# Hybrid decoder trunk: gate matmuls in fewer portions, keys and diagonal solves at later steps, T1's four products piece by piece

## The chip, the core and the metric

The kernel runs on one core of one Trainium2 chip. The metric is the device time in microseconds (us) of one execution. The core has a matrix engine (TensorE, here PE, whose weight loads are listed as PEld), VectorE (DVE), ScalarE (ACT), GpSimd (POOL) and SyncE (SP, which here only issues DMAs). Each engine works through its own list of instructions in a fixed order and waits on semaphores for the others.

## The reference

One layer of a decoder on 512 prompt tokens and 8 sample tokens, all in float32, model width 2048:

```
xn = rmsnorm(h);  proj = xn @ w_in            # q | k | v | z | beta logits | decay logits | pool channels
q, k, v = silu(short_conv(...)); l2norm(q), l2norm(k)
beta = sigmoid(b_raw);  g = -exp(a_log) * softplus(a_raw + dt_bias)
o = gated delta rule(q, k, v, cumsum(g), beta)   # per head: unit lower triangular solve in each chunk
h = h + [rmsnorm(o) * silu(z) ; multiscale_pool(p)] @ w_out
xn2 = rmsnorm(h);  gu = xn2 @ w_gate_up
h = h + (silu(gu[:, :5632]) * gu[:, 5632:]) @ w_down
y = rmsnorm(h)
```

For the prompt the delta rule is computed in chunks: the decay logits g are cumulated along the tokens, a triangular matrix of key products is built for each head and chunk, and it is inverted. The sample tokens use the stored states. The new states are outputs too.

## The kernel before

**Products in three passes.** The activations stand as columns (channels on partitions, 520 tokens along the free axis). Each float32 operand is cut into a high and a low part (ACT writes the high part by a cast, DVE the low part by a subtraction: lines L146 and L148, and L1222 and L1223 later), and a product is three matmuls, high x high, high x low, low x high (L179 to L181, and in the second half L1229 to L1231 in `passes`). A product of one output tile with 16 tiles of depth is done for two halves of the tokens (264 and 256 columns) that alternate on PE, the second three tiles behind the first (`product`, L183).

**Banks.** PSUM is split into two pools: `ps_mm` with three banks for the accumulators of the big products (L79) and `ps_dn` with five banks for the rest (L80, `pst()`).

**The weave.** In the first half, small work is woven between the matmuls of the big products: `Weave` (L43) has two tracks, each a list of tasks written as generators. `product` calls `weave.step()` after each pair of half steps in which both halves are at work, and once at its end, which makes 16 steps for a product of depth 16; a step in the middle of a product has six matmuls between it and the next. A task's `yield n` lets it rest for n steps; the next task of its track begins in the step in which the one before ends, but not before its own delay. Track 1 holds, in this order, `gates()` (L560), `keys(h)` for heads 0 to 3 with a delay of 16 each (L769), `eliminate(0)` (L803), and later the same for heads 4 to 7. Heads 0 and 1 have their key products behind them when the tracks start, so the steps run through the key products of heads 2 and 3, then the z-products (`z_tile`, L1023), then the q and v products (`qv_tiles`, L1096), which add `delta(h)` (L825) to track 0. Only PE's order is that of the program in this half (L531); the other engines' lists are made when the kernel is planned, from what is estimated to be ready and, among that, by place in the program, with the casts of weights and the evictions put ahead. So an engine can be given work of a later stage early, and then holds to that order.

- `gates()`: matmuls of the beta and decay logits (L566, L567: 64 of them, weights of 32 columns), a yield after every four depth tiles, 2 steps, transposes (L574), a chain on DVE and ACT (L580 to L611, result `gtok`, in the profile `sc_g`), 13 steps, matmuls that cumulate it (L616 to L618, L627), a row per head written to DRAM (L630), 4 steps, a last small matmul (L641).
- `keys(h)`: the decay tile `dm` of the head (`decay`, L752: a DMA of the head's row to all partitions into `gcb`, DVE L758, an exponential on ACT L760; both tiles are of tag `g3`, of which there are three), the key products and transposes on PE (L775, L778), sums of squares on ACT (L766), a power on POOL (L226), scaled products on DVE (L790, L792), a yield of 4 for heads 0 to 2 and of 2 for the others, and then four DMAs that write the diagonal blocks of 32 x 32 to DRAM (L797) and four memsets of them on POOL (L800).
- `eliminate(b)`: reads the diagonal blocks of four heads (L806, tile `nb`), clears `u` on POOL (L809, L810), solves all 64 blocks at once by 31 pairs of DVE operations (L815, L817), and writes the result to DRAM (L818, L821).
- `z_tile(h)`: a product whose accumulators ACT evicts with a Silu (L1027).
- `delta(h)`: uses `decay(h)` again (L758, L760, and a second exponential, L831), and the solved blocks, read back into `utf` (L1100), on PE from L839 on; POOL copies a part (L843).

**The second half** is ordered by hand on all engines (L1439). It computes the products with Strassen's scheme: forms of the activations (B11, B21, B22, T1 to T4) are made piece by piece by `stream` (L1604), two depth tiles at a time: DVE makes the piece, ACT its high part (L1598), DVE its low part (L1602). The first two pairs of output tiles of w_gate_up (weights `w0`, `w1`) are computed plainly while the forms are being made. Around the change PE runs: a0 and a1 (products with B11, copied out by L1709 and L1720), h0 (with B21), then four products with T1 (weights A11 and A21 of `w0` into `c0[0]`, `c0[1]`, those of `w1` into `c1[0]`, `c1[1]`, L1727 to L1731), then six products with B22 and B21 (L1736 to L1747) of 24 matmuls each, and then the first steady pair `gu[2]` with its products M1 (A11 with B11), M4 (A22 with T4), M7 and so on. On DVE and ACT the same stretch of the program holds the streams of T1, B22, T3, T2 and T4 (L1718 to L1755), the cuts of the weights (`gu[1].cut("A12")` L1733, `place` L1735, `gu[2].cut("A11")` L1742, `gu[2].cut("A22")` L1758) and the outputs of the first pairs (`gate_out`, L1395, `up_out`, L1399).

Of the kernel before, what the change touches and what calls it, by code (L numbers as in the profile page):

```python
# [69 lines left out]
def decoder_kernel(ctx, tc, x_prompt, x_sample, state_delta, state_conv, state_pool, norm_mix, w_in,  # L70
# [15 lines left out]
    c1 = c1s.enter_context(tc.tile_pool(name="c1", bufs=1, side="right"))  # L86

    def pst():
        return ps_dn.tile([P, 512], F32, tag="dn", name="dn")
# [118 lines left out]
    def part(hk, half, k0=0, k1=8):  # L208
        return (mixa, mixb)[hk][:, k0:k1, HALF * half:HALF * half + HALF]
# [14 lines left out]
    def pow_mhalf(out, src):  # L224
        n = src.shape[0]
        pool.tensor_tensor(out, src, mhalf[:n, :src.shape[1]], op=ALU.pow)  # L226
# [303 lines left out]
    with ExitStack() as p1:  # L530
# [4 lines left out]
        def d1tile(tag, shape, name, dtype=F32):  # L535
            return (pre if tag == "ext" else d1).tile(shape, dtype, tag=tag, name=name, bufs=BUFS[tag])
# [23 lines left out]
        def gates():  # L560
            take = scratch("aq", "g3")
            bas = d1tile("s0", [32, NTOK], "bas")
            for c0, c1 in CHUNKS:
                pa = pst()[:32, :c1 - c0]
                for k in range(KT):
                    te.matmul(pa, wba[:, k, :], xh[:, k, c0:c1], start=(k == 0), stop=False)  # L566
                    te.matmul(pa, wba[:, k, :], xl[:, k, c0:c1], start=False, stop=(k == KT - 1))  # L567
                    if k % 4 == 3:
                        yield 1
                dve.tensor_copy(bas[:, c0:c1], pa)  # L570
            yield 2
# [5 lines left out]
            with tc.high_priority(offset=AHEAD):  # L577
# [27 lines left out]
                for c in (15.0, 13.0, 11.0, 9.0, 7.0, 5.0, 3.0):  # L605
# [4 lines left out]
                act.activation(al, al, AF.Exp)  # L610
                dve.scalar_tensor_tensor(gtok, ax, -1.0, al.rearrange("p (o h) -> p o h", o=1).broadcast_to([P, 5, H]),  # L611
                                         op0=ALU.mult, op1=ALU.mult)
            yield 13
            g4 = gtok[:, 0:4, :].rearrange("p c h -> p (c h)")
            pg = pst()
            te.matmul(pg[:, 0:32], triu, g4, start=True, stop=True)  # L616
# [112 lines left out]
        def v3(a):  # L729
            return a.rearrange("p (c j) -> p c j", c=NCH)  # L730

        def bc3(a):
            return a.rearrange("p (c o) -> p c o", o=1).broadcast_to([P, NCH, P])

        def ck(c):
            return slice(P * c, P * (c + 1))
# [15 lines left out]
        def decay(h):  # L752

            gcb = d1tile("g3", [P, SEQ], "gcb")
            sp.dma_start(gcb, gcr_d[h:h + 1, :].broadcast_to([P, SEQ]))
            dm = d1tile("g3", [P, SEQ], "dm")
            for c in range(NCH):
                dve.scalar_tensor_tensor(dm[:, ck(c)], gcb[:, ck(c)], gcs[:, c, h:h + 1], mneg,  # L758
                                         op0=ALU.subtract, op1=ALU.min)
            act.activation(dm, dm, AF.Exp)  # L760
            return gcb, dm

        def squares(src, ss):
            junk = d1tile("junk", [P, P], "junk")
            for c in range(NCH):
                act.activation(junk, src[:, ck(c)], AF.Square, accum_out=ss[:, c:c + 1])  # L766


        def keys(h):  # L769
            kT, nn = mixb[:, h % 4, 0:SEQ], mixb[:, 4 + h % 4, 0:SEQ]  # L770
            kd = kds[h] = d1tile("kd", [P, SEQ], "kd")
            _, dm = decay(h)
            gp_ = pst()
            for c in range(NCH):
                te.matmul(gp_[:, ck(c)], kT[:, ck(c)], kT[:, ck(c)], start=True, stop=True)  # L775
            ktp = pst()
            for c in range(NCH):
                te.transpose(ktp[:, ck(c)], kT[:, ck(c)], ident)  # L778
            ss = d1tile("ss", [P, NCH], "ss")
            squares(ktp, ss)  # L780
            dve.tensor_scalar(ss, ss, EPS, None, op0=ALU.add)
            rr = d1tile("rr", [P, NCH], "rr")
            pow_mhalf(rr, ss)
            fk, ik, ad = sck[:, h, 0, :], sck[:, h, 1, :], sck[:, h, 2, :]
            dve.tensor_tensor(fk, rr, rr, op=ALU.mult)
            dve.tensor_tensor(fk, fk, btok[:, 0:4, h], op=ALU.mult)
            dve.tensor_tensor(ik, ss, rr, op=ALU.mult)
            dve.tensor_tensor(ad, fk, edec[:, :, h], op=ALU.mult)
            for c in range(NCH):
                dve.scalar_tensor_tensor(nn[:, ck(c)], gp_[:, ck(c)], fk[:, c:c + 1], dm[:, ck(c)],  # L790
                                         op0=ALU.mult, op1=ALU.mult)
            dve.tensor_tensor(v3(kd), v3(ktp), bc3(ad), op=ALU.mult)  # L792
            yield 4 if h < 3 else 2
            nn3 = v3(nn)
            for q in range(4):
                r = slice(32 * q, 32 * q + 32)
                sp.dma_start(nd_d[h, q].rearrange("c s j -> s c j"), nn3[r, :, r])  # L797
            for q in range(4):
                r = slice(32 * q, 32 * q + 32)
                pool.memset(nn3[r, :, r], 0.0)  # L800


        def eliminate(b):  # L803
            hs = slice(4 * b, 4 * b + 4)
            nb = d1tile("nb", [64, 32, 32], "nb")
            sp.dma_start(nb.rearrange("p s j -> p (s j)"), nd_d[hs].rearrange("h q c s j -> (h q c) (s j)"))  # L806
            u = d1tile("u", [64, 32, 32], "u")
            uf = u.rearrange("p s j -> p (s j)")
            pool.memset(uf, 0.0)  # L809
            pool.memset(uf[:, 0:1024:33], 1.0)  # L810
            for t in range(31, 0, -1):
                w = 32 - t
                tm = d1tile("tm", [64, 256], "tm")
                tv = tm[:, 0:t * w].rearrange("p (s j) -> p s j", j=w)
                dve.tensor_tensor(tv, nb[:, 0:t, t:t + 1].broadcast_to([64, t, w]),  # L815
                                  u[:, t:t + 1, t:32].broadcast_to([64, t, w]), op=ALU.mult)
                dve.tensor_tensor(u[:, 0:t, t:32], u[:, 0:t, t:32], tv, op=ALU.subtract)  # L817
            sp.dma_start(ud_d[hs, :, 0].rearrange("h q c s j -> (h q) c (s j)"), uf)  # L818
            ut = d1tile("nb", [64, 32, 32], "ut")
            dve.tensor_copy(ut, u.rearrange("p s j -> p j s"))  # L820
            sp.dma_start(ud_d[hs, :, 1].rearrange("h q c s j -> (h q) c (s j)"), ut.rearrange("p s j -> p (s j)"))  # L821
            yield 1
# [285 lines left out]
        for b in range(2):  # L1108
            for h in range(4 * b, 4 * b + 4):
                qkv_tile(1, h, mixb[:, h % 4, 0:SEQ],  # L1110
                         {0: ext_first, 1: ext_second}.get(h))
                if h == 0:
                    weave.add(states())
                    weave.add(gates(), 1)
                weave.add(keys(h), 1, 16)
            weave.add(eliminate(b), 1)
            for h in range(4 * b, 4 * b + 4):
                z_tile(h)
            for h in range(4 * b, 4 * b + 4):
                qv_tiles(h)  # L1120
# [105 lines left out]
    def passes(acc, w, form, start=True, stop=True, ks=None):  # L1226
        (wh, wl), (xf, xg) = w, forms[form]
        for k in ks or range(wh.shape[1]):
            te.matmul(acc, wh[:, k, :], xf[:, k, :], start=start and k == 0, stop=False)  # L1229
            te.matmul(acc, wh[:, k, :], xg[:, k, :], start=False, stop=False)  # L1230
            te.matmul(acc, wl[:, k, :], xf[:, k, :], start=False, stop=stop and k == wh.shape[1] - 1)  # L1231
# [161 lines left out]
    def gate_out(i, half, a, b):  # L1393
        c = slice(HALF * half, HALF * half + HALF)
        dve.tensor_tensor(sg[:, i, c], a, b, op=ALU.add)  # L1395
        act.activation(sg[:, i, c], sg[:, i, c], AF.Silu)
# [207 lines left out]
    def stream(name, src, make, lag=1):  # L1604

        for i in range(4 + lag):
            if i < 4:
                make(2 * i)
                high(name, src, 2 * i)
            if i >= lag:  # L1610
                low(name, src, 2 * (i - lag))

    def minus(dst, a, b):
        def make(k):
            r = slice(k, k + 2)
            dve.tensor_tensor(dst[:, r, :], a[:, r, :], b[:, r, :], op=ALU.subtract)

        return make
# [64 lines left out]
    c0 = [ps_mm.tile([P, HALF], F32, tag="mm", name="mm") for _ in range(2)]  # L1683
    a0 = two()
    halves = slice(0, HALF), slice(HALF, NTOK)
    w0, w1 = gu[0].w, gu[1].w
# [37 lines left out]
    stream("B22", part(1, 1), lambda k: normed(1, 1, k, k + 2))  # L1724
    for j in range(2):
        gate_out(j, 0, sg[:, j, halves[0]], h0[j])
    passes(c0[0], w0["A11"], "T1", stop=False)  # L1727
    passes(c0[1], w0["A21"], "T1", stop=False)
    c1 = [ps_mm.tile([P, HALF], F32, tag="mm", name="mm"), pst()[:, :HALF]]
    passes(c1[0], w1["A11"], "T1", stop=False)  # L1730
    passes(c1[1], w1["A21"], "T1", stop=False)  # L1731
    stream("T3", part(0, 1), minus(part(0, 1), part(1, 1), part(0, 1)))
    gu[1].cut("A12")  # L1733
    gu[2].load("A22")
# [350 lines left out]
```

## Time and profile before

| What | us |
|---|---|
| median of three runs | 2163.61 |
| lowest and highest run | 2163.47, 2163.62 |
| the profiled execution's own time | 2163.7 |
| its span (first to last instruction) | 2161.9 |
| PE busy in it | 2135.7 |

The profile is of one execution. A row of the timeline gives the start in us from the span's start, the duration (of the whole group where instructions are merged, with their count behind an x), the engine, the line, the operation, what it writes and reads, and in brackets how long the engine had been idle before and what ended that. A row of the waits gives who waited for whom, the sum in us, how often, and the longest. Matmuls overlap, so their distance is read from start to start. `SPq` rows are DMAs being issued.

### The profile page before, as it was taken

How to read it: one execution, taken by the hardware profiler on the slowest of the kernel's cores; microseconds unless marked ns; L12 is line 12 of the kernel's file. 1: busy time of each engine (PE TensorE's matmuls, PEld its weight loads, DVE VectorE, ACT ScalarE, POOL GpSimd, SP SyncE). 2: the span in 40 equal slices, each digit the busy share in tenths (PEclk: the TensorE clock that was granted, in tenths of full speed). 3: DMA queues.
4: the chain of work that ended last, by engine and by line, in shares of the span. 5: the costliest groups of instructions: out<-in, count | busy, mean ns of one | idle time of the engine just before them, and what ended most of it. 6: DMA issues, size and time to landing. Idle time of an engine off the chain costs nothing.

```text
span 2161.9 us, 42973 instructions
## 1 busy us (share of the span) xinstructions
PE 2135.7 (99%) x17809; PEld 2128.0 (98%) x17809; DVE 1719.7 (80%) x2517; ACT 952.2 (44%) x1493; POOL 439.6 (20%) x517
## 2 busy tenths in 40 slices
PE   7999999999999999999999999999999999999998
PEld 7999999999999999999999999999999999999998
DVE  7675657656499979988889888888877898887997
ACT  6534553443264545434334334434434444435544
POOL 2201120111012212233233233232013302003100
PEclk9999999999999999999999999999999999999999
DMA  8343233323445543555455554554446746438333
GB/s 263 96 111 94 81 96 102 96 77 82 131 125 152 152 128 108 147 161 148 142 162 148 146 161 146 144 164 135 129 139 189 240 107 208 115 103 251 89 108 119
DMA packets 443808, 297.03 MB, mean 137 GB/s; under 512 B 26540, under 2 KB 424773, under 8 KB 440269
## 3 DMA queue, kind: packets, MB, share of 16 engines
q1 hardware_dynamic: 424653, 220.87, 36.4%
q0 software_dynamic: 17968, 72.77, 10.4%
q8 instruction: 139, 2.28, 0.4%
q10 hardware_dynamic: 992, 0.66, 0.1%
q14 instruction: 56, 0.46, 0.1%
HBM read 251.47 MB, written 43.43 MB: 136 GB/s over the span
## 4 chain that ended last, share of the span: by engine, by line
PE 91%; DVE 5%; ACT 1%; issue 1%; DMA 1%; POOL 0%; DVEq 0%; POOLq 0%; ACTq 0%
PE dn L1229 21%; PE dn L1230 21%; PE dn L1231 21%; PE mm L179 7%; PE mm L180 7%; PE mm L181 7%; DVE lo L1223 1%; PE dn L858 1%; DMA st<-a_d 1%; DVE raw L1251 0%; POOL st L1784 0%; PE dn L968 0%; PE dn L865 0%; PE dn L775 0%; PE dn L904 0%
## 5 line engine op out<-in xcount | busy, mean ns | idle before, releaser
L1222 ACT CAST hi<-raw 128x1024 fp32r<-128x1024 f32 (+1 forms) x422 | 427.6, 1027 | 406.0 <-DVE raw L1251 209.7
L1223 DVE TENSOR_TENSOR lo<-raw,hi 128x1024 fp32r<-128x1024 f32 (+1 forms) x422 | 525.2, 1265 | 89.5 <-ACT hi L1222 85.9
L179 PE MATMUL mm<-xh,hi 128*128 128x256 f32 (+1 forms) x1280 | 379.5, 297 | 2.3 <-ACT mixa L1027 1.4
L180 PE MATMUL mm<-xl,hi 128*128 128x256 f32 (+1 forms) x1280 | 362.0, 283 | 2.5 <-DVE xl L360 2.1
L181 PE MATMUL mm<-xh,lo 128*128 128x256 f32 (+1 forms) x1280 | 361.9, 283 | 0.0
L180 PEld LDWEIGHTS mm<-xl,hi 128*128 128x128 f32 x1280 | 242.1, 189 | 3.6 <-DVE xl L360 2.9
L179 PEld LDWEIGHTS mm<-xh,hi 128*128 128x128 f32 x1280 | 241.6, 189 | 3.4 <-ACT mixa L1027 1.6
L181 PEld LDWEIGHTS mm<-xh,lo 128*128 128x128 f32 x1280 | 241.0, 188 | 0.0
L1251 DVE TENSOR_TENSOR raw<-raw 128x1024 f32<-128x1024 f32 (+1 forms) x130 | 173.8, 1337 | 2.2
L1229 PE MATMUL dn<-b21h,hi 128*128 128x260 f32 x620 | 175.5, 283 | 0.0
L1231 PE MATMUL dn<-b21h,lo 128*128 128x260 f32 x620 | 175.5, 283 | 0.0
L1230 PE MATMUL dn<-b21l,hi 128*128 128x260 f32 x620 | 175.0, 282 | 0.4 <-DVE b21l L1794 0.4
L1231 PE MATMUL dn<-b11h,lo 128*128 128x260 f32 x612 | 173.5, 283 | 1.7 <-DVE lo L1223 1.7
L1229 PE MATMUL dn<-b11h,hi 128*128 128x260 f32 x612 | 173.3, 283 | 0.0
L1230 PE MATMUL dn<-b11l,hi 128*128 128x260 f32 x612 | 172.6, 282 | 0.0
L148 DVE TENSOR_TENSOR lo<-raw,hi 128x1024 fp32r<-128x1024 f32 (+2 forms) x86 | 101.8, 1187 | 80.7 <-ACT hi L146 80.5
L1229 PE MATMUL dn<-T1h,hi 128*128 128x260 f32 x556 | 157.9, 284 | 0.0
L1230 PE MATMUL dn<-T1l,hi 128*128 128x260 f32 x556 | 157.7, 284 | 0.0
L1231 PE MATMUL dn<-T1h,lo 128*128 128x260 f32 x556 | 156.7, 282 | 0.0
L1229 PE MATMUL dn<-B22h,hi 128*128 128x260 f32 x548 | 155.2, 283 | 0.0
L1230 PE MATMUL dn<-B22l,hi 128*128 128x260 f32 x548 | 155.0, 283 | 0.0
L1231 PE MATMUL dn<-B22h,lo 128*128 128x260 f32 x548 | 154.1, 281 | 0.4 <-DVE lo L1223 0.4
(658 smaller groups left out, 6414.3 us busy)
## 6 DMA issues: line engine op xcount, KB each, us to landing
raw<-in_w_gate_up_dram SPq DMA_DIRECT2D x134, 512.0 KB
raw<-in_w_in_dram SPq DMA_DIRECT2D x80, 512.0 KB
a_d<-mixa POOLq DMA_DIRECT2D x22, 1040.0 KB, 5.5
raw<-in_w_down_dram SPq DMA_DIRECT2D x48, 448.0 KB
mixb<-in_w_gate_up_dram SPq DMA_DIRECT2D x41, 512.0 KB
raw<-in_w_out_dram SPq DMA_DIRECT2D x25, 512.0 KB
st<-a_d POOLq DMA_DIRECT2D x49, 260.0 KB, 6.4
raw<-in_w_down_dram SPq DMA_DIRECT2D x24, 512.0 KB
```

The lines of the kernel that those rows point to most:

```text
L148: dve.tensor_tensor(lo[:, r], raw[:, r], hi[:, r].bitcast(F32), op=ALU.subtract)
L179: te.matmul(acc[ci], wh, hi[k][:, c0:c1], start=(k == 0), stop=False)
L180: te.matmul(acc[ci], wh, lo[k][:, c0:c1], start=False, stop=False)
L181: te.matmul(acc[ci], wl, hi[k][:, c0:c1], start=False, stop=(k == len(w) - 1))
L858: te.matmul(yp[0:96, c, j], xt_[:, c, :], udf[:, c, j] if it == 0 else v3(cur)[:, c, j], start=True, stop=True)
L1222: act.copy(hi, raw)
L1223: dve.tensor_tensor(lo, raw, hi.bitcast(F32), op=ALU.subtract)
L1229: te.matmul(acc, wh[:, k, :], xf[:, k, :], start=start and k == 0, stop=False)
L1230: te.matmul(acc, wh[:, k, :], xg[:, k, :], start=False, stop=False)
L1231: te.matmul(acc, wl[:, k, :], xf[:, k, :], start=False, stop=stop and k == wh.shape[1] - 1)
L1251: dve.tensor_tensor(r[name], r[a], r[b], op=op)
```

## The change

Four edits. The logits' matmuls come in four portions of eight depth tiles and not in eight of four, and the cumulation comes 18 steps after the transposes and not 13. The writing out of a head's diagonal blocks, and with it the next head's keys, comes six steps after the head's products for heads 0 to 2, and not four. The elimination rests for six steps between the load of its blocks and its memsets and DVE operations. And the four products with T1 no longer run one after the other over all eight depth tiles: each piece of two depth tiles is used by all four, then the next piece; the two accumulators `c1` are therefore made before the first of the four.

```diff
@@ gates
-                    if k % 4 == 3:
+                    if k % 8 == 7:
                         yield 1
...
-            yield 13
+            yield 18
@@ keys
             dve.tensor_tensor(v3(kd), v3(ktp), bc3(ad), op=ALU.mult)
-            yield 4 if h < 3 else 2
+            yield 6 if h < 3 else 2
@@ eliminate
             uf = u.rearrange("p s j -> p (s j)")
+            yield 6
             pool.memset(uf, 0.0)
@@ the four products with T1
-    passes(c0[0], w0["A11"], "T1", stop=False)
-    passes(c0[1], w0["A21"], "T1", stop=False)
     c1 = [ps_mm.tile([P, HALF], F32, tag="mm", name="mm"), pst()[:, :HALF]]
-    passes(c1[0], w1["A11"], "T1", stop=False)
-    passes(c1[1], w1["A21"], "T1", stop=False)
+    for k in range(0, 8, 2):
+        for acc, wk in zip(c0 + c1, (w0["A11"], w0["A21"], w1["A11"], w1["A21"])):
+            passes(acc, wk, "T1", stop=False, ks=range(k, k + 2))
```

## The prediction

> **What bounds the kernel now.** I read the page first, then the waits of TensorE (PE), then the timeline around each of its waits, and last the waits of the two engines that feed it there.
>
> ```profile
> span 2161.9 us, 42973 instructions
> PE 2135.7 (99%) x17809; PEld 2128.0 (98%) x17809; DVE 1719.7 (80%) x2517; ACT 952.2 (44%) x1493; POOL 439.6 (20%) x517
> ...
> PE   7999999999999999999999999999999999999998
> ...
> PEclk9999999999999999999999999999999999999999
> ```
>
> PE works 99% of the span at the full granted clock in every slice. The change removes and adds no matmul, so it can only touch the 26 us (2161.9 - 2135.7) in which PE stands; the first and the last slice, which are below nine tenths, hold most of these, and no edit reaches there. The waits of PE show which ones lie at the edits:
>
> ```profile
> PE mm L179 <- ACT mixa L1027: 1.4, 1, 1.4
> PE mm L1230 <- DVE T1l L1602: 1.4, 2, 1.0
> ...
> PE dn L616 <- DVE sc_g L611: 0.8, 1, 0.8
> ```
>
> Three waits, each in reach of one edit. A row counts only idle time; what a wait costs is the distance between two starts less the normal distance, which the next rows show as 0.12 us.
>
> **Part 1, the gates.** The matmuls for the logits (L566, L567) stand between product matmuls; the cumulative sums (L616) wait for DVE.
>
> ```profile
> 61.86 0.28 PE L181 MATMUL mm<-xh,lo 128*128 128x256 f32 x1
> 61.98 0.28 PE L566 MATMUL dn<-xh,wba 128*32 128x256 f32 x1
> ...
> 80.24 0.28 PE L181 MATMUL mm<-xh,lo 128*128 128x256 f32 x1
> ...
> 81.34 0.41 PE L616 MATMUL dn<-sc_g,triu 128*128 128x32 f32 x2 [0.82 <-DVE sc_g L611]
> ```
>
> Going from a product to the logits costs the ordinary 0.12 (61.98 - 61.86), so eight portions or four are the same work: 0. By the yields, counted in weave steps, the old order is portions in steps 1 to 8, the copy in 9, then 2 and 13 steps: transposes in step 11, cumulation in 24. The new one is portions in 1 to 4, the copy in 5, then 2 and 18: transposes in 7, cumulation in 25. A full step is six product matmuls, 6 x 0.12 = 0.72 us. DVE's chain thus gets five steps more, 3.6 us at most, some of them half steps, and was late by 0.8. The wait goes: 81.34 - 80.24 - 0.12 = 1.0 us. What is late next is the first head's keys, one step later, which no PE wait shows near.
>
> **Part 2, keys six steps apart.** The yield stands between a head's products and the writing out of its diagonal blocks (four DMAs on SP, four memsets on POOL). As the tasks of a track follow each other, it moves the matmuls of heads 0, 1 and 2 from steps 28, 32 and 36 to 29, 35 and 41: by one (the gates' share), three, and five, 3.6 us. Head 3's stay, since the delay of 16 sets step 48 both times. No PE work changes. The DMAs are passed by weight loads that were queued behind them on SP; only the elimination after head 3 reads them. The PE wait nearby is a wait of z-tiles for a PSUM bank:
>
> ```profile
> 95.12 1.05 PE L775 MATMUL dn<-mixb 128*128 128x128 f32 x8
> ...
> 106.14 1.12 DVE L790 SCALAR_TENSOR_TENSOR mixb<-dn,sck,dm 128x128 f32<-128x128 f32 x4
> ...
> 110.04 0.36 SPq L755 DMA_DIRECT2D gcb<-gcr_d  x1
> ...
> 113.88 0.35 DVE L758 SCALAR_TENSOR_TENSOR dm<-gcb,gcs,mneg 128x128 f32<-128x128 f32 x1 [3.20 <-DMA gcb<-gcr_d]
> ...
> 115.30 0.29 PE L181 MATMUL mm<-xh,lo 128*128 128x264 f32 x1
> ...
> 116.98 0.63 ACT L760 ACTIVATE dm<-dm 128x512 f32<-128x512 f32 x1 [3.69 <-DVE dm L758]
> ...
> 118.15 1.28 ACT L1027 ACT_TABLE_LOAD   x1
> 118.17 0.28 PE L181 MATMUL mm<-xh,lo 128*128 128x264 f32 x1
> ...
> 119.44 0.67 ACT L1027 ACTIVATE mixa<-mm 128x264 f32<-128x264 f32 x2
> 119.89 0.38 PE L179 MATMUL mm<-xh,hi 128*128 128x256 f32 x1 [1.44 <-ACT mixa L1027]
> ```
>
> The z-product's first accumulator is complete at 115.6 (115.30 + 0.29), but its eviction runs at 119.44, because in ACT's fixed order an exponential stands ahead of it that belongs to the first head's delta stage, though that stage follows only after all z-products and the q and v products of that head. That decay tile takes one of three buffers of tag g3, free only when head 2's L790 (106.14) is done; then its load (110.04) and DVE (idle 3.20) follow. Price on PE: 119.89 - 118.17 - 0.12 = 1.6 us.
>
> Which comes first on ACT is settled when the kernel is planned, by what is ready. Head 2's products now come up to 3.6 us later, so the buffer, the load and the exponential become ready later too, while the eviction is ready at its PE time. In the old order the exponential had to be ready between the cast that precedes it and 115.6; moved 3.6 us later in that window it falls behind the eviction more likely than not. I take the wait as gone, 1.6 us; behind the eviction the exponential has about one z-product of room before PE needs the next bank. Ends: 1.6 gained; or more lost, if it still stands ahead (rivals).
>
> **Part 3, diagonal blocks later.** Six steps (from step 50 to 56 in the first block) between the elimination's load on one side, and its two memsets on POOL and 62 DVE operations on the other.
>
> ```profile
> 126.60 0.20 DVE L815 TENSOR_TENSOR tm<-nb,u 64x31 f32<-64x31 f32 x1 [4.30 <-DMA nb<-nd_d]
> ...
> 161.58 0.70 POOL L843 COPY uu<-utf 128x512 f32<-128x512 f32 x1 [3.42 <-DMA utf<-ud_d]
> ...
> 166.40 1.03 PE L839 MATMUL dn<-utf,mixb 128*128 128x96 f32 x8
> ```
>
> The chain starts when its load has landed (126.60), not when its place in the program comes; only PE is ordered by hand here, and the weights' casts are put ahead by priority anyway. So 0. The upper bound: the chain slips by the full six steps, 4.3 us. Its product lands at 161.58 and PE wants it at 166.40, 4.8 later; with PE 2.6 us ahead the cover is 2.2, and 2.1 us would show. A gain is excluded: no PE wait lies there.
>
> **Part 4, T1's pieces shared.** Every engine is ordered by hand here.
>
> ```profile
> 803.99 0.28 PE L1229 MATMUL mm<-T1h,t4oh 128*128 128x260 f32 x1
> ...
> 805.42 0.39 PE L1230 MATMUL mm<-T1l,t4oh 128*128 128x260 f32 x1 [0.43 <-DVE T1l L1602]
> ...
> 806.62 1.47 DVE L1602 TENSOR_TENSOR T1l<-mixa,T1h 128x520 fp32r<-128x520 f32 x2
> ...
> 807.37 0.39 PE L1230 MATMUL mm<-T1l,t4oh 128*128 128x260 f32 x1 [0.97 <-DVE T1l L1602]
> ...
> 817.53 0.28 PE L1229 MATMUL mm<-B22h,hi 128*128 128x260 f32 x1
> ```
>
> Four products of 24 matmuls take 96 x 0.12 = 11.5 us; they took 13.5 (817.53 - 803.99). With each piece serving four products, it lasts 4 x 6 x 0.12 = 2.9 us: the second is wanted at 806.9 and is there at 805.4, the third and fourth are wanted at 809.8 and 812.6 and are there by 808.1 (806.62 + 1.47). So 2.0 us go here. The fourth accumulator is now written from 806.1 on, 8 us sooner. Its bank:
>
> ```profile
> 792.65 0.67 PE L1462 MATMUL dn<-dg,ones 128*128 128x260 f32 x2
> ...
> 796.70 1.20 ACT L1709 COPY sg<-dn 128x260 f32<-128x260 f32 x4
> ...
> 807.27 0.65 ACT L1720 COPY cm<-dn 128x260 f32<-128x260 f32 x2
> ```
>
> Five banks are in turn. The spread at 792.65 ran before a0's two banks were copied out (796.70), so it used a fifth, and three are free for the pair h0 and this accumulator: no wait. If it took one of a1's, PE would wait until 807.9, 1.8 us.
>
> Neither counts, for the next wait takes the 2.0 back. Seven products of 24 matmuls later the first steady pair begins its second product (M4):
>
> ```profile
> 834.93 1.05 ACT L1222 CAST hi<-raw 128x1024 fp32r<-128x1024 f32 x1
> ...
> 837.14 1.22 DVE L1223 TENSOR_TENSOR lo<-raw,hi 128x1024 fp32r<-128x1024 f32 x1
> ...
> 837.81 0.28 PE L1230 MATMUL dn<-T4l,hi 128*128 128x260 f32 x1
> ...
> 838.42 0.39 PE L1231 MATMUL dn<-T4h,lo 128*128 128x260 f32 x1 [0.32 <-DVE lo L1223]
> ```
>
> M4's third matmul waits for the low part that DVE ends at 838.36. Would DVE be earlier if PE were? Its waits from 804 to 838.4, all of them, and the first and last of ACT's seven:
>
> ```profile
> DVE lo L1223 <- ACT hi L1222: 1.7, 2, 1.4
> DVE T4l L1602 <- ACT T4h L1598: 0.2, 1, 0.2
> ...
> ACT T2h L1598 <- DVE mixb L1616: 3.4, 3, 2.1
> ...
> ACT hi L1222 <- DVE mixa L1251: 1.1, 1, 1.1
> ```
>
> DVE waits only for ACT and ACT only for DVE; neither waits for PE. Their order stays, so 838.36 stays relative to the stage's start. PE gets to M4 at 835.7, runs two matmuls after the high part (834.93 + 1.05 = 836.0) and stands until 838.42: 2.0 - 2.0 = 0, and the bank's 1.8 would vanish in the same place.
>
> A rule of the Trainium skill speaks against this order: "TensorE: Matmul & The Clock Gate", section "Why this matters for your kernels", asks for K-contiguous loops and no idle gaps above about 3 us, else the clock falls to half. By it the four-way order alone would not matter as long as PE stays fed; the profile agrees, with all slices at 9 and two accumulators alternating in every product at 0.12. By the sum M4's gap stays under 3 us.
>
> **The sum.** -1.0 (gates) -1.6 (eviction) + 0 (elimination) -2.0 + 2.0 (T1, M4) = -2.6 us. The profiled execution took 2163.7, its span and 1.8 around it, 0.1 above the median of 2163.61; so 2161.1 there and **2161.0** as a median, 0.12% less. A measurement of this kernel can tell about 0.2%, 4.3 us.
>
> **Rivals.**
> - *The wait for the eviction stays.* For: heads 1 to 3 keep DVE and POOL busy to 107 and the old exponential came just ahead. ACT's 119.44 then rests on DVE and a DMA, not on PE, and the gates' 1.0 is eaten with it: 2163.6; if part of the lateness goes, 2162 to 2163. Against: head 2 moves away. 0.22.
> - *T1's gain is kept.* If the low part came early too: another -2.0, 2159.0. Against: the waits just quoted. 0.08.
> - *Slower:* the exponential stays ahead of the eviction and its load comes five steps later. It cannot start before head 2's product is used, so 119.44 becomes up to 123.0, and everything behind it is 3.6 us late: 2167.2. It decides from the point where the planner still sees it ready before 115.6. 0.10.
> - *The half clock:* if four-way accumulation counted as idling, T1's 96 matmuls would go at half the speed, 11.5 us more, 9.5 more than before: 2170.5. The row of granted clocks speaks against it. The page of the Trainium skill named above states that mechanism. 0.01.
> - *The elimination slips:* 2163.1 by the bound of part 3. 0.05.
>
> **Numbers.** The forecast has 0.51; the rest (0.03) are small new waits of ACT or DVE. Forecast, staying wait and slip hold 0.78, so I reach down to the kept gain: 2158.8 to 2164.6. Faster by over 0.2% (under 2159.3) needs the kept gain: 0.07. Slower by over 0.2% (above 2167.9) needs the slower rival with more on top, or the clock: 0.05. The rest, 0.88, is within.
>
> **What would show it.** Right: no PE row that waits for sc_g; none for mixa near 118 and, on ACT, the Silu eviction ahead of the early exponential; none for T1l, 96 T1 matmuls in 11.5 us; and one long wait, about 2.2 us, at L1231 for a low part some 20 us after T1. Wrong: if that last wait is absent while T1's are gone, DVE was not the bound and 2159 holds; if mixa still appears, part 2 failed; if L839 shows a wait for utf, part 3 did.

## The result and the profile after

The kernel with the change takes 2167.52 us, the median of 17 executions, where the kernel before took 2163.63 (17 executions): a ratio of 1.0017, 95% interval 1.0010 to 1.0024. The forecast was 2161.0 with a range up to 2164.6, so the result lies outside it, on the slow side. (One of the 17, at 2961 us and a mean clock of 0.655, was disturbed and isn't in the ratio; the other 16 lie between 2165.59 and 2170.30, with a median of 2167.4.) A second series of 11 gave 2167.59, ratio 1.0015 (1.0006 to 1.0024).

The profiled execution of the changed kernel took 2166.34 us. First its page, span and PE's row, then its waits of PE, those at the edits:

```profile
span 2164.6 us, 42974 instructions
PE 2136.6 (99%) x17809; PEld 2128.3 (98%) x17809; DVE 1721.4 (80%) x2517; ACT 953.3 (44%) x1493; POOL 438.7 (20%) x517
```
```profile
PE dn L1232 <- DVE lo L1224: 4.0, 5, 1.9
PE mm L179 <- ACT mixa L1028: 3.7, 2, 3.5
```

PE's work is the same and the wait for `sc_g` has no row any more, as forecast, nor has the one for `T1l`. But the wait for `mixa`, which was to vanish, went from 1.4 us to 3.5. Lines from L810 on are one higher than in the kernel before. The timeline there, ACT with PE, the columns being start, duration, engine, line, operation, and in brackets the idle time before it and what ended it:

```profile
119.21 0.63 ACT L760 ACTIVATE dm<-dm 128x512 f32<-128x512 f32 x1 [5.20 <-DVE dm L758]
119.75 0.61 ACT L832 ACTIVATE gcb<-gcb 128x512 f32<-128x512 f32 x1
120.38 1.28 ACT L1028 ACT_TABLE_LOAD   x1
121.67 0.67 ACT L1028 ACTIVATE mixa<-mm 128x264 f32<-128x264 f32 x2
```
```profile
118.35 0.28 PE L181 MATMUL mm<-xh,lo 128*128 128x264 f32 x1
122.12 0.39 PE L179 MATMUL mm<-xh,hi 128*128 128x256 f32 x1 [3.49 <-ACT mixa L1028]
```

The exponential of the first head's delta stage (L760) still stands ahead of the Silu eviction (L1028) on ACT, and it is later: ACT stands 5.2 us for DVE's `dm`. PE pays 122.12 - 118.35 - 0.12 = 3.65 us where it paid 1.6. DVE and the load show why it is late:

```profile
111.48 0.35 DVE L758 SCALAR_TENSOR_TENSOR dm<-gcb,gcs,mneg 128x128 f32<-128x128 f32 x1
...
111.81 1.12 DVE L790 SCALAR_TENSOR_TENSOR mixb<-dn,sck,dm 128x128 f32<-128x128 f32 x4
...
115.28 1.12 DVE L790 SCALAR_TENSOR_TENSOR mixb<-dn,sck,dm 128x128 f32<-128x128 f32 x4
116.31 0.68 DVE L792 TENSOR_TENSOR kd<-dn,sck 128x512 f32<-128x512 f32 x1
116.91 0.87 DVE L758 SCALAR_TENSOR_TENSOR dm<-gcb,gcs,mneg 128x128 f32<-128x128 f32 x3
117.70 1.22 DVE L148 TENSOR_TENSOR lo<-raw,hi 128x1024 fp32r<-128x1024 f32 x1
118.83 0.35 DVE L758 SCALAR_TENSOR_TENSOR dm<-gcb,gcs,mneg 128x128 f32<-128x128 f32 x1
```
```profile
111.85 0.34 SPq L755 DMA_DIRECT2D gcb<-gcr_d  x1
```

The scaled products of heads 2 and 3 (the two L790 rows) now follow each other 3.5 us apart, where they were 8.8 apart (106.14 and 114.97). The delta stage's four operations stand behind both, and the last of them behind a weight's low part as well. Its load is issued at 111.85, when head 3's last L758 has just ended (111.48 + 0.35): so the buffer comes back with that operation or an earlier one, and not with head 2's L790, which still runs.

(With the gates' edit alone the two L790 rows are already 4.4 us apart, at 110.45 and 114.89, and the exponential starts at 119.21 as well; the section on the prediction comes back to this.)

Where the 2.7 us between the two profiled spans (2164.6 and 2161.9) lie is read from four PE instructions of both timelines, as distances:

| From, to (starts of PE) | before | after | difference |
|---|---|---|---|
| span's start, first logits matmul (L566) | 53.60 | 54.44 | +0.84 |
| first L566, first product with `utf` (L839, L840) | 112.80 | 114.19 | +1.39 |
| that product, first T1 matmul | 637.59 | 638.07 | +0.48 |
| first T1 matmul, L1957 near the end | 1338.06 | 1338.04 | -0.02 |

No edit reaches the first row; the runs below have 53.5 to 54.5 there, with no pattern by their edits. The second row, which I call the woven stretch, is the measure for the first three edits, since it doesn't depend on the start.

### The profile page after: what moved, and what is told of

The parts are those of the page before. It is cut to its first block, busy times and chain, and to the rows that moved or that the text cites. A ratio compares the mean times of both kernels' runs of the same rounds, so it can differ in the third digit from the quotient of the medians.

```text
span 2164.6 us, 42974 instructions
## 1 busy us (share of the span) xinstructions
PE 2136.6 (99%) x17809; PEld 2128.3 (98%) x17809; DVE 1721.4 (80%) x2517; ACT 953.3 (44%) x1493; POOL 438.7 (20%) x517
## 4 chain that ended last, share of the span: by engine, by line
PE 89%; DVE 6%; ACT 2%; DMA 1%; issue 1%; POOL 0%; ACTq 0%; DVEq 0%; SPq 0%; POOLq 0%
PE dn L1230 21%; PE dn L1231 21%; PE dn L1232 21%; PE mm L179 7%; PE mm L180 7%; PE mm L181 7%; DVE lo L1224 1%; PE dn L859 1%; DMA st<-a_d 1%; DVE raw L1252 0%; DVE xl L206 0%; DVE lo L148 0%; ACT hi L1223 0%; PE dn L969 0%; PE dn L866 0%
## 5 line engine op out<-in xcount | busy, mean ns | idle before, releaser
L1224 DVE TENSOR_TENSOR lo<-raw,hi 128x1024 fp32r<-128x1024 f32 (+1 forms) x422 | 530.6, 1278 | 88.7 <-ACT hi L1223 86.0
```

The lines of the kernel that those rows point to most:

```text
L1224: dve.tensor_tensor(lo, raw, hi.bitcast(F32), op=ALU.subtract)
```

## The experiments

My theory after the result, E: PE pays for the place of the delta stage's exponential on ACT, which the keys' yields put ahead of an eviction and late. Its rivals: the gates' moves (G), T1 and M4 (M), late keys in themselves (K); the texts on record say what each expects. All runs are full kernels, each timed 11 times beside the kernel before. The columns are the median, the ratio with its interval (on record, against the kernel before in the same series, whose medians were 2163.66 to 2164.43; it isn't the quotient of two medians), the woven stretch, PE's idle time at that z-eviction and at M4's third matmul, all but the first two from one profiled execution.

| Run | median | ratio (95%) | woven stretch | z-eviction | M4 |
|---|---|---|---|---|---|
| before | 2163.6 | | 112.80 | 1.44 | 0.32 |
| gates alone | 2162.01 | 0.9993 (0.9984 to 1.0001) | 109.97 | none | 0.35 |
| keys alone | 2166.15 | 1.0008 (1.0000 to 1.0017) | 113.88 | 2.53 | 0.37 |
| T1 alone | 2164.84 | 1.0003 (0.9994 to 1.0012) | 112.60 | 1.24 | 1.89 |
| elimination alone | 2163.83 | 1.0000 (0.9991 to 1.0009) | 112.61 | 1.25 | 0.34 |
| whole, without keys | 2162.14 | 0.9992 (0.9984 to 1.0001) | 109.97 | none | 1.89 |
| whole change, again | 2167.59 | 1.0015 (1.0006 to 1.0024) | 116.41 | 3.36 | 1.89 |
| whole, load in an own buffer | 2163.78 | 0.9999 (0.9990 to 1.0007) | 111.77 | 1.55 | 1.89 |
| whole, both tiles in own buffers | 2166.28 | 1.0011 (1.0003 to 1.0020) | 110.44 | none | 1.89 |
| whole, keys eight apart | 2168.12 | 1.0019 (1.0010 to 1.0028) | 114.97 | none | 1.88 |
| whole, exponential forced behind | 2162.22 | 0.9991 (0.9982 to 1.0001) | 110.64 | none | 1.89 |
| gates, T1, A22 cut early | 2163.25 | 0.9995 (0.9986 to 1.0004) | 109.97 | none | none |
| gates, T1, S3 on POOL | 2163.06 | 0.9996 (0.9987 to 1.0005) | 109.97 | none | 0.75 |

The 116.41 of the whole change's second profile has some 2.7 us of half clock in it, as shown below.

### The edits one by one

**Gates alone.**

```diff
-                    if k % 4 == 3:
+                    if k % 8 == 7:
-            yield 13
+            yield 18
```

> Only the gates' edit (four portions, cumulation six yields later); keys, elimination and T1 as before. Theory E (the loss is the eviction of the z-tile near 119 us, behind the delta stage's exponential on ACT, and comes from the keys' yields): in the planned order of ACT the eviction now stands ahead of that exponential, so the wait for sc_g (0.8 us idle, 1.0 between starts) and the wait for mixa (1.4 idle, 1.6) both go: about 2161 us. Theory G (moving the logits' matmuls and the cumulation costs on its own): 2165 us or more, with a longer wait of PE before 170 us. Theory M (the loss hangs on T1 and the gap at M4): no loss here, 2162.6 to 2163.6 us.

Measured: 2162.01 us, and the stretch is 2.83 us shorter. ACT's timeline:

```profile
115.34 0.39 ACT L1027 ACTIVATE mixa<-mm 128x264 f32<-128x264 f32 x1
...
119.21 0.63 ACT L760 ACTIVATE dm<-dm 128x512 f32<-128x512 f32 x1
```

The Silu eviction runs at 115.34, ahead of the delta stage's exponential at 119.21, and PE has no wait there. So the gates' edit, which moves the keys by one step, was enough for the whole gain in this stretch that I had forecast for gates and keys together (1.0 + 1.6). The exponential is as late as in the whole change (119.21 in both profiles); only its place in ACT's order differs.

**Keys alone.**

```diff
-            yield 4 if h < 3 else 2
+            yield 6 if h < 3 else 2
```

> Only the keys' yields (six instead of four). Theory E: in ACT's planned order the delta stage's exponential still stands ahead of the z-tile's eviction, and it can only start when the third head's products are through; PE's wait for mixa grows from 1.4 us to about 3.5, the wait for sc_g stays at 0.8, and the time is about 2165.7 us. Theory G: as before, 2163.6. Theory M: as before, 2163.6, and no lower granted clock.

```profile
119.50 0.63 ACT L760 ACTIVATE dm<-dm 128x512 f32<-128x512 f32 x1 [5.31 <-DVE dm L758]
120.15 1.28 ACT L1027 ACT_TABLE_LOAD   x1
121.44 0.67 ACT L1027 ACTIVATE mixa<-mm 128x264 f32<-128x264 f32 x2
```

Measured: 2166.15 us; in ACT's timeline the exponential is ahead and late, and PE waits 2.53 us, less than the 3.5 expected, at the same place. The stretch is 1.1 us longer.

**T1 alone** (the last hunk of the change).

> Only T1's four products in turn over pairs of pieces. Theory E: the waits for T1l (1.4 us in all) go and the wait for the low part at M4's third matmul grows from 0.3 to about 2.3 us, net nothing: 2163.6 us, granted clock as before. Theory M: the loss of the whole change is here, 2165 us or more, through the longer gap at M4 or a lower clock after it.

Measured: no wait for `T1l`, 1.89 us idle at M4. The median, 2164.84, is 1.2 above that of before, in an interval that includes no change. The profile has the lower clock of theory M behind M4's gap, to which I return below.

**The elimination alone** (`yield 6` ahead of its memsets).

> Only the elimination's six yields. By the prediction and by the run without the keys' edit it costs nothing: PE waits for nothing of it (utf, uu), the stretch from the first logits matmul to the product with utf stays at 112.8 us, 2163.6 us. If the elimination slips by its six steps, a wait at the utf or uu product of up to 2.1 us and 2165.7.

Measured: 2163.83 us, no wait at `utf` or `uu`. It costs nothing.

**The whole change without the keys' edit.**

> The whole change without the keys' yields (four as before). Theory E: ACT's planned order has the eviction ahead of the delta stage's exponential; no wait for sc_g, none above 0.5 us for mixa near 119, M4's wait about 2.2: about 2161 us, below before by the 2.6 us that were forecast for the whole change. Theory G or M: as the whole change or nearly, 2165 to 2167.5 us.

Measured: 2162.14 us and a woven stretch of 109.97, as with the gates alone. So the keys' yields turn a gain of 2.8 us in that stretch into a loss of 1.4, and everything else in the change together does what the gates do.

### Is it the exponential's place, or are late keys dear in themselves?

**A buffer of its own for the delta stage's load.** `decay` is given tags; for head 0's delta `gcb` takes tag `aq`, which is free there. The run has one edit more: in a later stage, that of the pool channels, a tile `dh` takes tag `g3` in place of `vs`. What that alone does wasn't measured; the rows below all lie ahead of that stage.

```diff
-            gcb, dm = decay(h)
+            gcb, dm = decay(h, ("aq", "g3")) if h == 0 else decay(h)
...
-                tags = ("ext", "ext") if gi == 3 else (("aq", "vs"), ("qts", "xt_"))[gi % 2]
+                tags = ("ext", "ext") if gi == 3 else (("aq", "g3"), ("qts", "xt_"))[gi % 2]
```

> The whole change, but the load for the first head's delta stage (gcb) has a buffer of its own and no longer waits until the third head's scaled products free one of the three of tag g3; ACT's order near 118 us is as in the whole change, the exponential ahead of the z-tile's eviction. Theory E (PE waits there because that exponential rests on the buffer, then the load, then DVE): without the load in the chain the exponential comes 2 to 4 us earlier, PE's wait for mixa falls from 3.5 us to under 1, and the time is 2162 to 2164 us. Theory K (the later keys cost by themselves, by their own place on PE, DVE and ACT, whoever owns the buffer): the wait stays above 3 us and the time at 2166 to 2167.5.

```profile
116.67 0.64 ACT L760 ACTIVATE dm<-dm 128x512 f32<-128x512 f32 x1 [3.51 <-DVE dm L758]
117.21 0.61 ACT L832 ACTIVATE gcb<-gcb 128x512 f32<-128x512 f32 x1
117.84 1.28 ACT L1028 ACT_TABLE_LOAD   x1
119.14 0.67 ACT L1028 ACTIVATE mixa<-mm 128x264 f32<-128x264 f32 x2
```

Measured: 2163.78 us. ACT's order is the same, but the exponential starts 2.5 us earlier (116.67, where the whole change had 119.21), so does the eviction, and PE's wait shrinks by 1.94. I expected under 1 us; 1.55 is left, since DVE's operations still lie between those of head 3. PE's wait follows the exponential. (The text on record has the buffer freed by head 2's scaled products; by the rows of the whole change it is back before these have ended.)

**Both tiles in buffers of their own** (`("aq", "vs")`).

> The whole change, but both decay tiles of the first head's delta stage (gcb and dm) have buffers of their own, so that neither waits for the keys of another head; the exponential then stands well ahead on ACT and its data are there. Theory E: no wait for mixa above 0.5 us near 119 and about 2162 us, as without the keys' edit. Theory K: 2166 to 2167.5 us.

```profile
169.95 0.61 POOL L844 COPY uu<-utf 128x512 f32<-128x512 f32 x1 [4.25 <-DMA utf<-ud_d]
170.50 0.10 POOL L270 MEMSET ext<- 128x3 f32 x1
170.55 1.01 POOL L226 TENSOR_TENSOR fq<-ss,mhalf 128x4 f32<-128x4 f32 x1
```

Measured: the exponentials are done by 110.8 and the woven stretch is 110.44, as expected, but the time is 2166.28, as theory K said. POOL's timeline shows the reason: a copy for the second head waits 4.25 us for its load, the power for the first head (L226) stands behind it, DVE waits 3.1 us for that power, and PE waits 2.5 for DVE, after the end of the stretch, with a granted clock of 0.58 and 0.56 from 172 to 176. From the product with `utf` to the first T1 matmul this execution takes 641.98 us, the others 637.25 to 638.96. The gain is given to another wait, of the same kind, and to the half clock at it.

**Keys eight apart.**

```diff
-            yield 6 if h < 3 else 2
+            yield 8 if h < 3 else 2
```

> The whole change, with keys eight steps apart in place of six. ACT's planned order now has the z-tile's eviction ahead of the delta stage's exponential. Theory E (the order on ACT decides, not how late the keys are): no wait for mixa above 0.5 us at that eviction, about 2162 us, so that eight steps are faster than six; a smaller wait further on, where the exponentials now stand ahead of the next evictions, may take up to 2 us back. Theory K: later keys cost more, so slower than the whole change, 2168 us or more.

```profile
163.79 0.63 ACT L749 ACTIVATE qT<-y 128x512 f32<-128x512 f32 x1 [11.62 <-DVE y L748]
164.33 1.03 ACT L146 CAST hi<-raw 128x1024 fp32r<-128x1024 f32 x1
165.38 1.28 ACT L760 ACT_TABLE_LOAD   x1
166.67 0.63 ACT L760 ACTIVATE dm<-dm 128x512 f32<-128x512 f32 x1
167.21 0.61 ACT L832 ACTIVATE gcb<-gcb 128x512 f32<-128x512 f32 x1
167.73 0.35 ACT L275 COPY ext<-mm 128x256 f32<-128x256 f32 x1
```

Measured: 2168.12 us. The wait at the z-eviction is gone, but 3.75 us appear at a later eviction: there the copy L275 stands behind a Silu that waits for DVE and behind the next head's exponentials. My 2162 was wrong: I had looked at one place of the plan, and the plan changes everywhere. By its time this run can't tell E from K; by its rows it is the same mechanism at another bank.

**The exponential forced behind.** The decisive run. One element of the second z-tile's output is copied by POOL into `gcb` ahead of its load, so that the delta stage's decay can't come before that eviction; the keys stay six apart.

```diff
             gcb = d1tile("g3", [P, SEQ], "gcb")
+            if behind is not None:
+                pool.tensor_copy(gcb[:, 0:1], behind)
...
-            gcb, dm = decay(h)
+            gcb, dm = decay(h, mix[1][:, 10:11] if h == 0 else None)
```

> The whole change with keys still six apart, and one small POOL copy of an element of the second z-tile's output into the delta stage's gcb tile before its load, which forces that load, DVE's four operations and the exponential behind the eviction. In ACT's planned order the eviction then stands ahead. Theory E (PE pays for the place of the exponential, not for the late keys): no wait for mixa near 119; PE from its first logits matmul to the product with utf takes 110.0 us as with the gates alone, not 114.2 as in the whole change; about 2162 us, up to 2 more if the later load makes another stage late, as two of the runs before showed. Theory K (late keys cost by themselves): 114 us in that stretch and 2166 to 2167.5 us.

```profile
114.87 0.39 ACT L1030 ACTIVATE mixa<-mm 128x264 f32<-128x264 f32 x1 [0.49 <-PE mm L181]
...
125.48 0.63 ACT L762 ACTIVATE dm<-dm 128x512 f32<-128x512 f32 x1 [6.58 <-DVE dm L760]
```

Measured: 2162.22 us, woven stretch 110.64. With the very yields of the whole change and one dependence more, the loss is gone: 5.3 us between the medians. Theory K falls; the place of the exponential on ACT is the cause. (The dependence moves its load and DVE's four operations too; that these being late isn't enough is shown by the gates alone, where the exponential starts at the same 119.21, behind the eviction, and PE doesn't wait.)

### Can T1's gain be kept?

**A22 cut ahead of T4's stream**, with the gates' and T1's edits.

```diff
+    gu[2].cut("A22")
     stream("T4", part(1, 0), minus(part(1, 0), part(1, 0), part(1, 1)))
...
-    gu[2].cut("A22")
```

> The gates' edit and T1's edit alone, and the cut of A22 of the first steady pair moved ahead of the stream of T4 in the order by hand, so that DVE makes the low part that M4 waits for before T4's pieces and not after. If the low part is what takes T1's gain back, M4's wait falls from 1.9 us to under 0.5 and the time is 2.0 us under that of the gates alone: about 2160.0 us. If something else is due there at the same time (T4's last low piece, ACT's casts), a wait of 1 us or more takes its place and the time stays at 2161.5 to 2162.

```profile
837.17 0.39 PE L1229 MATMUL dn<-T3h,hi 128*128 128x260 f32 x1 [0.59 <-ACT hi L1222]
...
838.43 0.39 PE L1231 MATMUL dn<-T3h,lo 128*128 128x260 f32 x1 [0.75 <-DVE lo L1223]
...
842.50 0.39 PE L1231 MATMUL dn<-T2h,lo 128*128 128x260 f32 x1 [0.95 <-DVE lo L1223]
...
852.08 0.39 PE L1231 MATMUL dn<-B22h,lo 128*128 128x260 f32 x1 [0.64 <-DVE lo L1223]
```

Measured: M4 runs without a wait, 2.5 us sooner after T1 than before. But the three products behind it wait, 0.59 + 0.75 + 0.95 + 0.64 = 2.9 us in all, each for the next weight's parts (of the last, 0.44 were there with the gates alone), and the time is 2163.25, not 2160. DVE is 93% busy from 804 to 874 (65.1 of 70 us with the gates alone): moving this cut only chose which product waits.

**S3 on POOL**, with the gates' and T1's edits.

```diff
-    gu[2].add("S3")
+    gu[2].add("S3", pool)
```

> The gates' and T1's edits, and the subtraction S3 of the first steady pair (1.22 us on DVE, just ahead of the low part for which M4 waits) done by POOL, which is idle there. If DVE's queue is what gives T1's gain back, M4's wait falls from 1.9 us to about 0.8, PE takes some 1.1 us less from T1 to the end, and the time is 1.1 us under that of the gates alone: about 2160.9 us. If ACT's cast of A22 or the load is as late as DVE, or POOL slows DVE, nothing is gained: 2162.

```profile
826.48 2.40 POOL L1251 TENSOR_TENSOR mixa<-raw,mixa 128x1024 f32<-128x1024 f32 x1 [36.82 <-DMA mixa<-in_w_gate_up_dram]
```
```profile
826.98 2.98 DVE L1223 TENSOR_TENSOR lo<-raw,hi 128x1024 fp32r<-128x1024 f32 x1 [1.43 <-ACT hi L1222]
```

Measured: 2163.06 us. M4's third matmul waits 0.75, as expected, but its first now waits 1.95 for ACT's cast. While POOL subtracts, DVE's low part beside it takes 2.98 us in place of 1.22, and ends 1.08 after POOL's operation (829.96 and 828.88): the 1.22 taken off DVE come back as 1.76. So whether DVE's queue alone was the bound isn't settled by this run; that POOL beside DVE doesn't relieve it is.

### The clock

> The whole change once more, for its clock. Its first profiled execution had 1.00 granted around both of its long gaps (3.5 us near 122, 1.9 us near 841), yet most of its executions show a mean clock of 0.995 to 0.997 and take 1 to 4 us more than that one. In five other runs with M4's gap of about 2 us the granted clock was 0.50 for some 3.4 us from that gap on. Theory C (each long gap of PE can drop the clock to half for 3.4 us, which costs up to 1.7 us and 0.0008 of the mean clock): this profile or the timed runs show it again, half clock right behind 122 or 841, and the times fall with the mean clock, 1 us for each 0.001. Theory S (the extra time is from the start of the program or from noise): no half clock behind those gaps whenever the mean clock is low, and no such slope.

Measured: 2167.59 us, and the profiled execution, at 2169.02, has the half clock at both gaps. Stretches of 2 us, with the busy time of each engine (and its instructions in brackets) and, third from the end, the granted clock; first this execution, then the first one of the same kernel, then T1 alone behind M4's gap:

```profile
120.00:122.00 2.00, 0.67 (x3) 0.67 (x4) 0.00 (x0) 1.99 (x4) 0.00 (x0) 0.67 0.92 259
122.00:124.00 2.00, 2.00 (x11) 2.00 (x11) 1.23 (x1) 0.48 (x1) 0.00 (x0) 0.50 0.68 157
124.00:126.00 2.00, 2.00 (x11) 2.00 (x10) 0.85 (x5) 0.00 (x0) 0.00 (x0) 0.50 0.47 123
126.00:128.00 2.00, 2.00 (x13) 2.00 (x12) 1.79 (x7) 0.00 (x0) 0.00 (x0) 0.62 0.51 150
```
```profile
124.00:126.00 2.00, 2.00 (x19) 2.00 (x18) 0.61 (x2) 0.00 (x0) 0.00 (x0) 1.00 0.18 40
```
```profile
838.00:840.00 2.00, 1.82 (x8) 1.82 (x9) 2.00 (x4) 0.00 (x0) 0.00 (x0) 0.52 0.00 0
```

At half clock PE issues 11 matmuls in 2 us, not 19, though it counts as busy all the time. From the end of the gap to the product with `utf` this execution took 49.25 us (170.58 - 121.33), the first one 46.51 (168.63 - 122.12): the clock costs 2.7 us beside the 3.4 us of the gap. The mean clock of the 16 and the 11 executions of the whole change goes with their times: medians of 2166.0 us at 0.999 (2 executions), 2166.2 at 0.998 (3), 2167.35 at 0.997 (6), 2168.1 at 0.996 (14) and 2169.9 at 0.995 (2), about 1 us for 0.001. The first profiled execution was thus one of the lucky ones, and I put the median's extra microsecond over it down to the clock. M4's gap of 1.9 us does the same in five of the eight profiles that have it at that length (for 3.4 us; not in the other three), and so does the gap of 1.95 us at M4's first matmul with S3 on POOL; none of the five profiles without a gap there shows a lower clock at that place.

## Why the prediction was wrong, and where it was right

**What bounds the kernel.** Right: the result lies in a handful of PE's waits. Wrong was "each in reach of one edit": the eviction's wait was in reach of the gates' edit too, and two edits acted on it against each other. "The full granted clock in every slice" was read too finely from the row: a slice is 54 us long, and the kernel before itself has 0.50 from 20 to 22 us in a slice that shows a 9.

**Gates: right, and understated.** -1.0 at the cumulation, as worked out: L616 now runs 0.12 behind the product ahead of it (81.89 and 81.77). Not seen: the gates' edit by itself moves the exponential behind the eviction, another 1.6.

**Keys: the step that failed.** "Moved 3.6 us later in that window it falls behind the eviction more likely than not" was argued as if later could only mean later in ACT's plan too. The plan is made from estimates; with six steps it puts the exponential first all the same, and in the execution its operations on DVE queue behind heads 2 and 3, which had come close together. For that lateness the keys' yields weren't needed: with the gates alone the exponential starts at 119.21 as well, and with the keys alone at 119.50, where it was 116.98 before. With the gates alone head 2's scaled products come at 110.45 and not at 106.14, although PE's key matmuls for that head start at 95.37 and not at 95.12, so it is the other engines' order that made them late. What the keys' yields decide is that the eviction stands behind. So -1.6 became +2.0 (3.65 - 1.6), 3.6 off the sum. The chain that I gave for the exponential (head 2's L790, then the load) was wrong in its first link for the changed kernel as well. Why the estimate has it first at six steps and, with the gates' edit, not at four or eight, I haven't found out.

**The slower rival was what happened.** It named this mechanism, this place and a price of up to 3.6 us, and 2167.2 us as the time; it had a chance of 0.10. The number came out near by another sum: the eviction's wait grew by 2.0, the gates' gain was kept, and the clock took its part. The first two alone make 2164.6 (2163.6 + 2.0 - 1.0). Of the other 2.9 us I put about 1.2 down to the clock, by the difference of the median from the first profiled execution; the start's 0.8, and 0.8 spread over the stretches, have no cause that I could show.

**Elimination: right**, 0, alone and in the whole change. The kernel after starts it at 125.92, before it was 126.60, and its product waits for nothing.

**T1: right in its mechanism and, in the profile, to a tenth of a us.** The 96 matmuls take 11.5 us (818.24 - 806.70) without a wait, no bank is missed, and M4's third matmul gives it back: 34.44 us from the first T1 matmul to it, 34.43 before. The two attempts to keep it show that the return wasn't a matter of one wait's place.

```profile
841.14 0.39 PE L1232 MATMUL dn<-T4h,lo 128*128 128x260 f32 x1 [1.89 <-DVE lo L1224]
```

**The half clock: the wrong trigger.** I gave it 0.01 and tied it to the four-way order. The 96 matmuls ran at full clock; it was the gaps that I had priced at their length alone, M4's among them, that brought it. A rule of the Trainium skill is weighed here a second time: "TensorE: Matmul & The Clock Gate", section "What's actually happening", has the clock fall after an idle window of about 3.4 us, on a window that runs freely. The traces agree in part: the low stretches last 3.4 us or twice that, and a gap of 3.4 or 3.5 us brings them in one execution of the kernel and not in the next. But so long an idle window isn't needed: at the single gap of 2.5 us with both tiles in own buffers, and at M4's, 2.6 us with two matmuls in it (835.29 + 0.28 to 838.18 in T1 alone), the clock fell as well; at the keys' own gap of 2.53 us it didn't. There the measurement decides.

## What to carry to other kernels

Where a planner orders the queues, a yield is not a shift of some steps but a new plan: look, in the order of each fixed queue, at what stands ahead of each eviction that PE waits for, and pin that order by a dependence where it matters, rather than trust that later work falls behind. A gap of PE of 2 to 4 us costs its own length and, in some executions, the half clock behind it, so price it as a range and compare medians, not two profiles. Of a gain that another engine's queue takes back, ask for that engine's load over the next tens of microseconds, not for the next wait.

## What the hardware showed beside that

POOL held DVE up: a 128x1024 subtraction of two SBUF tiles took DVE 2.98 us beside a POOL one, and 1.22 alone. The Trainium skill's "GPSIMD Engine Reference", section "1. Specifications", says that GpSimd's SBUF interfaces are shared with VectorE and that it contends with DVE instructions that have two SBUF inputs. The traces agree, and the kernel before showed it already:

```profile
678.66 1.68 POOL L1508 TENSOR_TENSOR sqa<-sqa,sq 128x520 f32<-128x520 f32 x1
```
```profile
679.08 2.34 DVE L1223 TENSOR_TENSOR lo<-raw,hi 128x1024 fp32r<-128x1024 f32 x1
```

DVE's operation ends at 681.42, 1.08 us after POOL's (680.34). Of the 54 low parts of that size that start in the kernel before while a POOL TENSOR_TENSOR has more than 0.2 us left to run, 52 end 1.08 or 1.09 us after it, which is as if DVE stood still until POOL was through. So the subtraction that went to POOL cost DVE 1.76 us, nearly the 1.9 that POOL's operation had left when DVE's began, for 1.22 taken off.

The best kernels of this study, at 2162.0 to 2162.2 us, all keep one part of the change, the gates' edit; none of them is told apart from the others, and against the kernel before their intervals end at 1.0001, so that none is shown to be faster than it.
